# The 20th up tile of each FFN by seven block products

## The chip, the cores and the metric

The kernel runs on one core of a Trainium2 chip. Its metric is the device time of one execution in microseconds, from the launch to the end, as the median of several runs. The core has five engines that each work through their own list of instructions in order: TensorE (PE) for matmuls, VectorE (DVE) and ScalarE (ACT) for elementwise work, GpSimd (POOL), and SyncE (SP), which issues most of the loads. They wait for each other through semaphores. A matmul reads its operands from SBUF and adds into PSUM.

## The reference

A decoder of two layers over 512 tokens of width 1024, all in float32. Each layer has a mixer, a gated FFN with a causal convolution of width 3, and a gated embedding. The change lies in the FFN, which comes once in each layer:

```python
D_MODEL = 1024
SEQ = 512
D_FF = 2816
CONV_WIDTH = 3
...
def conv_ffn(xn, w_up, conv_w, conv_b, w_down):
    """Gated MLP with causal depthwise conv (width 3) between up-projection and activation."""
    S = xn.shape[1]
    h = xn @ w_up
    hp = jnp.pad(h, ((0, 0), (CONV_WIDTH - 1, 0), (0, 0)))
    c = conv_b + sum(hp[:, t:t + S] * conv_w[t] for t in range(CONV_WIDTH))
    g, u = jnp.split(c, 2, axis=-1)
    return (jax.nn.silu(g) * u) @ w_down
```

`w_up` is 1024 x 5632: 2816 columns for the gate `g` and 2816 for the line `u`. `w_down` is 2816 x 1024.

## The kernel before

**Tiles.** Activations lie with features on the 128 partitions and the 512 tokens along the free axis. The FFN's 2816 hidden features are 22 tiles of 128, numbered from 0, so that the 20th is tile 19. An up tile computes 128 gate rows and 128 line rows from the eight feature blocks of the input. Every float32 operand is split into a high and a low half (`wh` and `wl` for weights), and a product is three matmuls: high by high, high by low, low by high (`mm3`, L234).

**Two forms of an up tile.** The plain form (`up`) is 2 x 8 x 3 = 48 matmuls of 512 columns, into two PSUM tiles `up`. The form by seven block products (`woven_up`) treats gate and line rows, pairs of feature blocks, and the two halves of the tokens as a 2 x 2 by 2 x 2 block matrix product and forms it with seven products where eight are usual. Each product is 4 x 3 matmuls of 256 columns, so 84 in all. They go into PSUM tiles `ux` and `uy`, in the order 1, 2, 6, 5, 7, 3, 4. Between them ScalarE copies `ux` out into `gate` and `line` (L790, L794, L550) and half of `uy` into `side` (L796); a product that adds to a PSUM tile again waits for that copy. VectorE then finishes `line` (L803) and `gate` (L804). For its operands it needs sums of weight blocks, which VectorE forms in `weave` (L163, wide, then L164 and L165, half as wide), and sums of input blocks, made once for an FFN.

**Weights.** SP loads the weights of an up tile (128 x 2048, 1 MB) into one of three staging buffers, used in turn, by L173 (`wraw`). A tile by block products takes the next buffer as well, for its sums (`wsum`). A buffer is free for the next load or sum when the last split out of it is done. The weights are then split in units of at most 1024 columns: ScalarE casts the high half (`wh`, L203), VectorE subtracts for the low half (`wl`, L204). A plain tile has two units of 1024; a tile by block products has three of 1024 (blocks, sums, sums) and one of 512. There are four `wh` and four `wl` buffers, so that a unit can be split when TensorE is done with the unit four before it. TensorE takes the units in order.

**After an up tile**, `gated` runs the convolution: ScalarE scales by one tap (`c`, L753), VectorE adds two taps for gate and two for line (L755), ScalarE takes the silu (L761), VectorE multiplies (L762), and the product is split by ScalarE and VectorE into `act` high (L311) and low (L312).

**Parts.** The 22 tiles are handled in three parts, 0 to 7, 8 to 15 and 16 to 21. After each part come the down products of that part's hidden features. In the last part tile 16 is computed during the down products before it, then tiles 17 to 21 follow one another, then the down products in the plain form: four chunks of 36 matmuls each, whose weights are 128 x 1536 each (`d`, `wraw<-in_w_down`). The first chunk takes `act` 16 to 20 for both of its PSUM tiles and only then `act` 21. The scheduler sets the order of the instructions on each engine from the program's order and its own estimates; the order stays fixed at run time.

**The tables.** `UPS` (L23) names the tiles by block products. `ASIDE` (L24) names those among them whose `gate` and `line` lie in a free activation buffer, by its number, and not in the two common ones (`hs`). `turn` (L141) says which of the three staging buffers the first load takes.

The lines that the change and the steps of the prediction touch, cut short:

```python
    def staged(name):
        tags = state["tags"]
        r = wp.tile([P, 2 * UNIT], F32, tag=f"r{tags[state['turn'] % len(tags)]}", bufs=1, name=name)
        state["turn"] += 1
...
        def up(j, later=False):
            if j in UPS:
                return woven_up(j, later)
...
            head, tail = (ap.tile([P, S], F32, tag=f"a{y}{ASIDE[j]}", name=f"{x}{j}") if j in ASIDE else
                          tp.tile([P, S], F32, tag="hs", name=f"{x}{j}") for x, y in (("gate", "h"), ("line", "l")))
```

Of the kernel before, what the change touches and what calls it, by code (L numbers as in the profile page):

```python
# [19 lines left out]
NJ = FF // P  # L20
PARTS = [(0, 8), (8, 16), (16, 22)]
WOVEN = 2
UPS = (8, 9, 10, 12, 14, 16, 17, 18, 20, 21)  # L23
ASIDE = {9: 7, 17: 7, 20: 6}  # L24
PAIRS = 4
SLOTS = 9
N = S // 2
# [25 lines left out]
def tile_yoco(ctx: ExitStack, tc: tile.TileContext, t, out: bass.AP, out_b: bass.AP):  # L53
# [13 lines left out]
    def psum(name):  # L67
        return mmp.tile([P, S], F32, tag="mm", name=name)
# [35 lines left out]
    def plan_ups(l, j0, j1):  # L104
        for j in range(j0, j1):
            (plan_woven if j in UPS else plan_cols)(t["w_up"][l, j : j + 1], 1, *((0, KD) if j in UPS else (KD,)))

# [30 lines left out]

    units = [(i, q, lo, n) for i, p in enumerate(pieces) for q, (lo, n) in enumerate(p[2])]
    raws, ready, splits, sums = {}, {}, {}, {}  # L140
    state = {"raw": 0, "unit": 0, "next": 0, "tags": [0, 1, 2], "turn": 3, "pt": 0, "sent": {}}  # L141

    def behind(ins, front):

# [578 lines left out]
    def ffn(l, norm, nxt):  # L723
# [6 lines left out]
# [3 lines that stand above are left out]
            parts = chunk(256, KD)  # L733
            pss = [psum(f"up{j}_{s}") for s in range(2)]
            if j:
                for s in range(2):
                    mm3(pss[s], parts, xs, s * P)
            else:
                for k, ((wh, wl, off), (xh, xl)) in enumerate(zip(parts, xs)):
                    for x, both in ((xh, (wh, wl)), (xl, (wh,))):  # L740
                        for s, ps in enumerate(pss):
                            for w in both:
                                nc.tensor.matmul(ps, w[:, off + s * P : off + (s + 1) * P], x,  # L743
                                                 start=k == 0 and x is xh and w is wh, stop=k == KD - 1 and x is xl)
            return pss if later else gated(j, pss)
# [34 lines left out]
        def woven_up(j, later):  # L780

            product = products(ins)
            n = PAIRS * P
            chain, other = psum(f"ux{j}")[:, first], psum(f"uy{j}")
            head, tail = (ap.tile([P, S], F32, tag=f"a{y}{ASIDE[j]}", name=f"{x}{j}") if j in ASIDE else
                          tp.tile([P, S], F32, tag="hs", name=f"{x}{j}") for x, y in (("gate", "h"), ("line", "l")))
            side = tp.tile([P, N], F32, tag="sq", name=f"side{j}")
            w = unit()
            product(1, chain, w, 0)
            behind(box["silu"], nc.scalar.copy(head[:, first], chain))  # L790
            product(2, other[:, first], w, n)
            w = unit()
            product(6, chain, w, 0, first=False)
            nc.scalar.copy(head[:, second], chain)  # L794
            product(5, other[:, second], w, n)
            nc.scalar.copy(side, other[:, second])  # L796
            w = unit()
            product(7, chain, w, 0, first=False)
            minus(tail[:, second], chain)
            product(3, other[:, second], w, n, first=False)  # L800
            product(4, chain, unit(), 0, first=False)
            minus(tail[:, first], chain)
            nc.vector.tensor_sub(tail[:, second], tail[:, second], side)  # L803
            nc.vector.tensor_add(head, head, other)  # L804
            return (head, tail) if later else gated(j, (head, tail))
# [821 lines left out]
```

## Time and profile before

| | |
|---|---|
| median of 3 runs | 1101.53 us |
| lowest, highest | 1100.87, 1101.94 us |
| the profiled execution, its own time | 1102.24 us |
| its span, first to last instruction | 1100.5 us |
| tiles 17 to 21 in the first FFN | 415.63 to 467.12 us |
| tiles 17 to 21 in the second FFN | 963.76 to 1015.24 us |
| granted TensorE clock, mean | 0.998 |

The busy line of the page gives for each engine its busy time, the share of the span and the number of instructions. The chain that ended last is followed back from the last instruction: its shares say which engine set the time. A view of waits says who waited for whom: total, times, longest, in us. A row in order of time has the start, the length, the engine, the line and the operation with its output and inputs, and in brackets the idle time before it and what ended that. Neighbours on VectorE and ScalarE overlap a little at start and end, and a matmul's length is its time through the array, so the start-to-start time says what an instruction costs.

### The profile page before, as it was taken

The page shows a single profiled execution, that of the slowest core. Times are in us where ns is not written, and L with a number is a line of the kernel's source. Part 1 is how long each engine was busy: PE and PEld are TensorE (multiplying, and loading weights), DVE is VectorE, ACT ScalarE, POOL GpSimd, SP SyncE. Part 2 cuts the span into 40 slices and gives each one's busy share as a digit, 9 for nine tenths or more (in the row PEclk, how much of TensorE's full clock was granted, in tenths as well). Part 3 has the DMA queues.
Part 4 walks back from the last instruction along what each step waited for, and adds up shares of the span by engine and source line. Part 5 has one row for each costly group of instructions (what it writes and reads, how often), then busy time and mean ns, then how long its engine had stood idle before and what let it go on. Part 6 is the DMA issues. An engine that isn't in the chain of part 4 may idle for free.

```text
span 1100.5 us, 17400 instructions
## 1 busy us (share of the span) xinstructions
PE 1091.2 (99%) x6557; PEld 973.3 (88%) x6557; DVE 934.4 (85%) x1490; ACT 667.4 (61%) x1163; POOL 155.9 (14%) x228
## 2 busy tenths in 40 slices
PE   9999999999999999999999999999999999999997
PEld 7888988889998999988888887888899989999886
DVE  5598789888799978877988997798887999798796
ACT  5745665556676656655656775565566666566544
POOL 1100300002200030021114442000022000300200
PEclk9999999999999999999999999999999999999999
DMA  8621784126833388353234226441278333974634
GB/s 299 127 91 43 195 270 144 49 77 137 190 115 116 91 175 252 124 187 111 67 87 134 78 58 228 174 153 39 77 162 164 116 115 92 205 221 144 201 95 96
DMA packets 52692, 151.32 MB, mean 137 GB/s; under 512 B 13624, under 2 KB 21568, under 8 KB 42112
## 3 DMA queue, kind: packets, MB, share of 16 engines
q1 hardware_dynamic: 40560, 128.77, 36.5%
q0 software_dynamic: 10480, 16.78, 10.1%
q10 hardware_dynamic: 1568, 4.65, 1.1%
q8 instruction: 51, 0.84, 0.3%
q14 instruction: 33, 0.27, 0.1%
HBM read 116.89 MB, written 25.18 MB: 129 GB/s over the span
## 4 chain that ended last, share of the span: by engine, by line
PE 93%; DVE 2%; DMA 2%; issue 1%; ACT 1%; SPq 0%; POOLq 0%; POOL 0%; ACTq 0%; DVEq 0%
PE up L234 22%; PE ux L234 10%; PE dx L234 10%; PE uy L234 8%; PE dy L234 7%; PE q L234 4%; PE gate L234 4%; PE u L234 4%; PE o L234 4%; PE d L234 3%; PE up L743 2%; PE pv L1316 1%; PE v L244 1%; PE v L246 1%; PE v L245 1%
## 5 line engine op out<-in xcount | busy, mean ns | idle before, releaser
L204 DVE TENSOR_TENSOR wl<-wraw,wh 128x1024 fp32r<-128x1024 f32 (+2 forms) x198 | 219.1, 1110 | 49.8 <-ACT wh L203 47.4
L203 ACT CAST wh<-wraw 128x1024 fp32r<-128x1024 f32 (+2 forms) x197 | 183.6, 938 | 110.6 <-PE up L234 26.1
L204 DVE TENSOR_TENSOR wl<-wsum,wh 128x1024 fp32r<-128x1024 f32 x80 | 97.8, 1227 | 38.9 <-ACT wh L203 37.3
L203 ACT CAST wh<-wsum 128x1024 fp32r<-128x1024 f32 x80 | 84.1, 1051 | 38.0 <-PE uy L234 12.9
L755 DVE SCALAR_TENSOR_TENSOR c<-up,vec,c 128x511 f32<-128x511 f32 (+1 forms) x96 | 71.2, 746 | 2.5 <-ACT c L753 1.9
L594 POOL DMA_DIRECT2D saved<-side x16 | 13.9, 870 | 401.2 <-ACT side L550 401.2
L234 PE MATMUL up<-nf10h,wh 128*128 128x512 f32 x176 | 68.5, 389 | 0.0
L234 PE MATMUL up<-nf00h,wh 128*128 128x512 f32 x176 | 68.5, 389 | 0.0
L234 PE MATMUL up<-nf10l,wh 128*128 128x512 f32 x176 | 68.5, 389 | 0.0
L234 PE MATMUL up<-nf00l,wh 128*128 128x512 f32 x176 | 68.5, 389 | 0.0
L234 PE MATMUL up<-nf00h,wl 128*128 128x512 f32 x176 | 68.4, 389 | 0.0
L234 PE MATMUL up<-nf10h,wl 128*128 128x512 f32 x176 | 68.2, 389 | 0.0
L753 ACT ACTIVATE c<-up,vec 128x512 f32<-128x512 f32 x48 | 37.0, 775 | 34.2 <-PE up L234 29.0
L163 DVE TENSOR_TENSOR wsum<-wraw 128x1024 f32<-128x1024 f32 x40 | 48.9, 1223 | 0.8
L234 PE MATMUL ux<-t,wh 128*128 128x256 f32 x240 | 45.8, 283 | 0.0
L234 PEld LDWEIGHTS up<-nf00h,wl 128*128 128x128 f32 x176 | 33.0, 188 | 6.9
L234 PEld LDWEIGHTS up<-nf10h,wl 128*128 128x128 f32 x176 | 33.0, 188 | 6.8
L234 PEld LDWEIGHTS up<-nf10l,wh 128*128 128x128 f32 x176 | 33.1, 188 | 6.8
L234 PEld LDWEIGHTS up<-nf00l,wh 128*128 128x128 f32 x176 | 33.0, 188 | 6.8
L234 PEld LDWEIGHTS up<-nf10h,wh 128*128 128x128 f32 x176 | 33.1, 188 | 6.6
L234 PEld LDWEIGHTS up<-nf00h,wh 128*128 128x128 f32 x176 | 33.0, 188 | 6.6
L234 PEld LDWEIGHTS ux<-t,wh 128*128 128x128 f32 x240 | 37.4, 192 | 0.0
(738 smaller groups left out, 3693.0 us busy)
## 6 DMA issues: line engine op xcount, KB each, us to landing
wraw<-in_w_up SPq DMA_DIRECT2D x44, 1024.0 KB, 5.5
wraw<-in_w_down SPq DMA_DIRECT2D x16, 1024.0 KB, 4.9
wraw<-in_w_gate SPq DMA_DIRECT2D x8, 1024.0 KB, 5.7
wraw<-in_w_down SPq DMA_DIRECT2D x8, 768.0 KB, 4.4
wraw<-in_w_u SPq DMA_DIRECT2D x4, 1024.0 KB, 9.4
wraw<-in_w_out SPq DMA_DIRECT2D x4, 1024.0 KB, 5.0
saved<-head POOLq DMA_DIRECT2D x16, 256.0 KB, 4.9
saved<-rest POOLq DMA_DIRECT2D x16, 256.0 KB, 7.4
```

Of the source, the lines that this page charges most:

```text
L163: nc.vector.tensor_add(s[:, 0::3], g[:, 1:2].to_broadcast([P, 2, k, P]), g[:, 0::3])
L203: cast = nc.scalar.copy(hi, src)
L204: state["split"] = splits[u] = cast, nc.vector.tensor_sub(low, src, hi.bitcast(F32))
L234: return [nc.tensor.matmul(ps, w, x, start=first and j == 0, stop=last and j == len(todo) - 1, skip_group_check=onto) for j, (w, x) in enu ...
L244: nc.tensor.matmul(ps, xh[:, s], wh[:, a:b], start=st, stop=False)
L245: nc.tensor.matmul(ps, xl[:, s], wh[:, a:b], start=False, stop=False)
L246: nc.tensor.matmul(ps, xh[:, s], wl[:, a:b], start=False, stop=en)
L594: box["onto"] = nc.gpsimd.dma_start(x, y, accum_op=ALU.add)
L743: nc.tensor.matmul(ps, w[:, off + s * P : off + (s + 1) * P], x, start=k == 0 and x is xh and w is wh, stop=k == KD - 1 and x is xl)
L753: nc.scalar.activation(c, ps, AF.Identity, bias=v("conv_b", l * 2 * NJ + col), scale=cw[2])
L755: ins = nc.vector.scalar_tensor_tensor(c[:, tap:], ps[:, : S - tap], cw[2 - tap], c[:, tap:], op0=ALU.mult, op1=ALU.add)
L1316: nc.tensor.matmul(ps, lhs, rhs, start=j == 0, stop=j == len(todo) - 1)
```

## The change

Tile 19 joins the tiles by block products, in both FFNs. With it all five tiles from 17 to 21 have that form. Tile 19 takes the aside buffer 6, and tile 20 moves from 6 to 7. As tile 19 now takes two staging buffers, the first turn is set one lower, so that what follows the first FFN meets the same buffers as before.

```diff
--- before.py
+++ after.py
@@ -20,8 +20,8 @@
 NJ = FF // P
 PARTS = [(0, 8), (8, 16), (16, 22)]
 WOVEN = 2
-UPS = (8, 9, 10, 12, 14, 16, 17, 18, 20, 21)
-ASIDE = {9: 7, 17: 7, 20: 6}
+UPS = (8, 9, 10, 12, 14, 16, 17, 18, 19, 20, 21)
+ASIDE = {9: 7, 17: 7, 19: 6, 20: 7}
 PAIRS = 4
 SLOTS = 9
 N = S // 2
@@ -138,7 +138,7 @@
 
     units = [(i, q, lo, n) for i, p in enumerate(pieces) for q, (lo, n) in enumerate(p[2])]
     raws, ready, splits, sums = {}, {}, {}, {}
-    state = {"raw": 0, "unit": 0, "next": 0, "tags": [0, 1, 2], "turn": 3, "pt": 0, "sent": {}}
+    state = {"raw": 0, "unit": 0, "next": 0, "tags": [0, 1, 2], "turn": 2, "pt": 0, "sent": {}}
 
     def behind(ins, front):
```

The scheduler orders the stretch anew. Three places follow; the rows are in the engine's order, and the number behind a name says which tile (`gate18`, `c17_0`: tile 18, tile 17, gate) or which unit (`wl123`) or load (`wraw46`, tile 19's in both) it is.

VectorE, first FFN, while TensorE is in tile 18, before: tile 17's line taps and product, tile 19's two units, then the sums of tile 20.

```order
L755 SCALAR_TENSOR_TENSOR c17_1_4566<-line17_4447,vec_84,c17_1_4566 128x511
L755 SCALAR_TENSOR_TENSOR c17_1_4566<-line17_4447,vec_84,c17_1_4566 128x510
L762 TENSOR_TENSOR a17_4570<-a17_4570,c17_1_4566 128x512
L204 TENSOR_TENSOR wl123_4622<-wraw46_4619,wh123_4621 128x1024
L312 TENSOR_TENSOR act17l_4574<-a17_4570,act17h_4573 128x512
L204 TENSOR_TENSOR wl124_4652<-wraw46_4619,wh124_4651 128x1024
L163 TENSOR_TENSOR wsum47_4684<-wraw47_4680 128x2x512
L803 TENSOR_TENSOR line18_4588<-line18_4588,side18_4589 128x256
L164 TENSOR_TENSOR wsum47_4684<-wsum47_4684,wraw47_4680 128x512
L204 TENSOR_TENSOR wl125_4683<-wraw47_4680,wh125_4682 128x1024
L165 TENSOR_TENSOR wsum47_4684<-wsum47_4684,wraw47_4680 128x512
L804 TENSOR_TENSOR gate18_4587<-gate18_4587,uy18_4586 128x512
```

The same place with the change:

```order
L755 SCALAR_TENSOR_TENSOR c17_1_4566<-line17_4447,vec_84,c17_1_4566 128x511
L163 TENSOR_TENSOR wsum46_4623<-wraw46_4619 128x2x512
L755 SCALAR_TENSOR_TENSOR c17_1_4566<-line17_4447,vec_84,c17_1_4566 128x510
L164 TENSOR_TENSOR wsum46_4623<-wsum46_4623,wraw46_4619 128x512
L762 TENSOR_TENSOR a17_4570<-a17_4570,c17_1_4566 128x512
L165 TENSOR_TENSOR wsum46_4623<-wsum46_4623,wraw46_4619 128x512
L204 TENSOR_TENSOR wl123_4622<-wraw46_4619,wh123_4621 128x1024
L312 TENSOR_TENSOR act17l_4574<-a17_4570,act17h_4573 128x512
L204 TENSOR_TENSOR wl124_4656<-wsum46_4623,wh124_4655 128x1024
L803 TENSOR_TENSOR line18_4588<-line18_4588,side18_4589 128x256
L804 TENSOR_TENSOR gate18_4587<-gate18_4587,uy18_4586 128x512
L204 TENSOR_TENSOR wl125_4685<-wsum46_4623,wh125_4684 128x1024
```

The three sums of tile 19 now stand between tile 17's taps, its product and the first unit; after that unit 124 is a split of sums, and the sums of tile 20 come only after tile 18's taps.

ScalarE, in the same place, before: a copy of tile 18, tile 17's `act`, unit 124, the copy `side18`, and on.

```order
L794 COPY gate18_4587<-ux18_4585 128x256
L311 CAST act17h_4573<-a17_4570 128x512
L203 CAST wh124_4651<-wraw46_4619 128x1024
L796 COPY side18_4589<-uy18_4586 128x256
L550 ACTIVATE line18_4588<-ux18_4585 128x256
L203 CAST wh125_4682<-wraw47_4680 128x1024
```

And with the change:

```order
L794 COPY gate18_4587<-ux18_4585 128x256
L203 CAST wh124_4655<-wsum46_4623 128x1024
L311 CAST act17h_4573<-a17_4570 128x512
L796 COPY side18_4589<-uy18_4586 128x256
L550 ACTIVATE line18_4588<-ux18_4585 128x256
L203 CAST wh125_4684<-wsum46_4623 128x1024
```

The cast of unit 124 now reads the sums and stands ahead of tile 17's `act`; both stand ahead of the copy `side18`.

ScalarE at the end of the part, before: unit 134 is the second half of the first down chunk's weights, 135 and 136 those of the second (`wraw50`).

```order
L794 COPY gate21_4928<-ux21_4926 128x256
L311 CAST act20h_4922<-a20_4919 128x512
L796 COPY side21_4930<-uy21_4927 128x256
L203 CAST wh134_4992<-wraw49_4960 128x768
L550 ACTIVATE line21_4929<-ux21_4926 128x256
L203 CAST wh135_5023<-wraw50_5021 128x768
L753 ACTIVATE c21_0_5042<-gate21_4928,vec_84 128x512
L550 ACTIVATE line21_4929<-ux21_4926 128x256
L203 CAST wh136_5061<-wraw50_5021 128x768
L753 ACTIVATE c21_1_5046<-line21_4929,vec_84 128x512
L761 ACTIVATE a21_5050<-c21_0_5042 128x512
L311 CAST act21h_5053<-a21_5050 128x512
```

With the change the numbers of the units are two higher (137 and 138 are the second chunk's, 139 and 140 the third's):

```order
L203 CAST wh137_5081<-wraw50_5079 128x768
L311 CAST act20h_4980<-a20_4977 128x512
L550 ACTIVATE line21_4987<-ux21_4984 128x256
L753 ACTIVATE c21_0_5100<-gate21_4986,vec_84 128x512
L753 ACTIVATE c21_1_5104<-line21_4987,vec_84 128x512
L203 CAST wh138_5119<-wraw50_5079 128x768
L761 ACTIVATE a21_5108<-c21_0_5100 128x512
L203 CAST wh139_5179<-wraw51_5177 128x768
L311 CAST act21h_5111<-a21_5108 128x512
L203 CAST wh140_5183<-wraw51_5177 128x768
```

The cast of the second chunk's first unit has moved ahead of `act20h`, of the last copy for `line21` and of both `c21`, and one unit of the third chunk stands ahead of `act21h`. On VectorE the order there is the same: the split of unit 137, `act20` low, the four taps of tile 21, unit 138, the product, unit 139, `act21` low; before, `act20` low and both units of the first chunk were done ahead of the second chunk's first unit, and the third chunk's first unit came after `act21` low. SP issues the third chunk's load (`wraw51`) ahead of the second's (`wraw50`) in both: the third goes into the buffer of tile 21's sums, the second into that of tile 21's weights, and the next tile's weights or sums always wait for the split before them in that buffer.

## The prediction

> **What bounds the kernel now.** I read the busy line first, then the chain that ended last and TensorE's waits, then the four stretches of the part in which the changed tile lies, and last that part's instructions one by one.
>
> ```profile
> PE 1091.2 (99%) x6557; PEld 973.3 (88%) x6557; DVE 934.4 (85%) x1490; ACT 667.4 (61%) x1163; POOL 155.9 (14%) x228
> PE 93%; DVE 2%; DMA 2%; issue 1%; ACT 1%; SPq 0%; POOLq 0%; POOL 0%; ACTq 0%; DVEq 0%
> ```
> ```profile
> PE idle L283 <- DVE minus_half L286: 1.1, 1, 1.1
> PE gt L246 <- DVE wl L204: 0.2, 1, 0.2
> PE sc L1248 <- PE sc L1249: 0.2, 1, 0.2
> ```
>
> TensorE is on 93% of the chain, and all its waits in 1100.5 us are these three, none of them in an FFN's last part. So time can come only from fewer or shorter matmuls, and every wait that the change makes for TensorE is paid in full, since no later idle time can take it up. VectorE is the one to watch. Stretches by rows (start:end, length, then busy time of PE, PEld, DVE, ACT, POOL): tiles 17 and 18, tile 19, tiles 20 and 21, the down products; tile 19 and tiles 20 and 21 again in the second FFN.
>
> ```profile
> 415.63:436.00 20.37, 20.37 (x171) 20.21 (x170) 18.95 (x25) 14.64 (x25) 1.75 (x2) 1.00 0.78 229
> 436.00:446.91 10.91, 10.91 (x50) 9.01 (x49) 10.17 (x14) 5.87 (x9) 0.00 (x0) 1.00 0.36 148
> 446.91:467.12 20.21, 20.21 (x169) 20.15 (x168) 17.81 (x25) 14.14 (x25) 0.41 (x2) 1.00 0.46 157
> 467.12:499.80 32.68, 32.68 (x147) 27.04 (x145) 23.94 (x30) 18.09 (x28) 6.71 (x5) 1.00 0.55 193
> 984.13:995.04 10.91, 10.91 (x51) 9.00 (x50) 10.16 (x14) 5.87 (x9) 0.00 (x0) 1.00 0.35 147
> 995.04:1015.24 20.20, 20.20 (x169) 20.14 (x168) 18.10 (x25) 14.36 (x25) 0.53 (x1) 1.00 0.46 154
> ```
>
> VectorE is busy 10.17 us of the plain tile's 10.91: it pays there what tiles 17 and 18 left over. The plain tile 19 is VectorE's rest, and the change takes it away.
>
> **TensorE's gain.** The plain tile is 48 matmuls of 512 columns, the block form 7 x 12 of 256. From the chain, in order of time (start, length):
>
> ```profile
> 436.16 10.91 PE up L234 x48
> 422.98 1.59 PE uy L234 x12
> 424.57 2.87 PE ux L234 x24
> ```
>
> Twelve of 256 take 1.44 us (2.87 for 24), so a block tile takes 7 x 1.44 = 10.05; where a product first waits for the copy of `side` it is 0.15 more (1.59). Tiles 20 and 21 together took 20.21. So the gain is 10.91 - 10.05 = 0.86 us at best, some 0.75 with that small wait, for each FFN: 1.5 to 1.7 us in all. [...]
>
> **VectorE's added work.** Start-to-start times are what counts, since neighbours overlap by some 0.09 us:
>
> ```profile
> 427.41 0.69 DVE L204 TENSOR_TENSOR wl<-wraw,wh 128x512 fp32r<-128x512 f32 x1
> 428.01 0.75 DVE L755 SCALAR_TENSOR_TENSOR c<-gate,vec,c 128x510 f32<-128x510 f32 x1
> 428.67 1.53 DVE L755 SCALAR_TENSOR_TENSOR c<-line,vec,c 128x511 f32<-128x511 f32 x2
> 430.31 0.69 DVE L762 TENSOR_TENSOR a<-a,c 128x512 f32<-128x512 f32 x1
> 430.92 1.22 DVE L204 TENSOR_TENSOR wl<-wraw,wh 128x1024 fp32r<-128x1024 f32 x1
> 433.89 1.22 DVE L163 TENSOR_TENSOR wsum<-wraw 128x1024 f32<-128x1024 f32 x1
> 435.02 0.42 DVE L803 TENSOR_TENSOR line<-line,side 128x256 f32<-128x256 f32 x1
> 435.36 0.68 DVE L164 TENSOR_TENSOR wsum<-wsum,wraw 128x512 f32<-128x512 f32 x1
> 435.96 1.22 DVE L204 TENSOR_TENSOR wl<-wraw,wh 128x1024 fp32r<-128x1024 f32 x1
> 437.10 0.68 DVE L165 TENSOR_TENSOR wsum<-wsum,wraw 128x512 f32<-128x512 f32 x1
> 437.70 0.68 DVE L804 TENSOR_TENSOR gate<-gate,uy 128x512 f32<-128x512 f32 x1
> 438.37 0.75 DVE L755 SCALAR_TENSOR_TENSOR c<-line,vec,c 128x511 f32<-128x511 f32 x1
> ```
>
> So a wide sum (L163) takes 1.13, a 1024 split 1.14, a 512 sum, split or product 0.60, a tap (L755) 0.66, L803 0.34, L804 0.67. Tile 19 gains one L163, an L164 and L165 (2.33 together), one and a half more splits (1.74) and L803 and L804 (1.01): 5.1 us. Its taps cost the same from either source. ScalarE gains 1.5 casts and five short copies, and has the idle time for them (5.87 busy of 10.91).
>
> Is VectorE late by that? From tile 17's line tap (428.67 in both orders) to the last split of tile 21's weights the new order has 10 taps (6.60), 3 L163 (3.39), 6 sums (3.60), 9 splits of 1024 (10.26) and 3 of 512 (1.80), 3 products and 3 `act` splits (3.60), 3 L803 (1.02) and 3 L804 (2.01): 32.28. Without one wait it ends at 428.67 + 32.28 + 0.09 = 461.04. Before:
>
> ```profile
> 458.64 0.69 DVE L204 TENSOR_TENSOR wl<-wraw,wh 128x512 fp32r<-128x512 f32 x1
> 459.36 0.33 SPq L173 DMA_DIRECT2D wraw<-in_w_down  x1
> 461.42 0.96 DVE L204 TENSOR_TENSOR wl<-wraw,wh 128x768 fp32r<-128x768 f32 x1
> 462.30 0.68 DVE L762 TENSOR_TENSOR a<-a,c 128x512 f32<-128x512 f32 x1
> 466.07 0.83 ACT L203 CAST wh<-wraw 128x768 fp32r<-128x768 f32 x1 [1.14 <-DMA wraw<-in_w_down]
> 473.14 0.69 DVE L312 TENSOR_TENSOR act21l<-a,act21h 128x512 fp32r<-128x512 f32 x1 [0.69 <-ACT act21h L311]
> 474.18 0.39 PE L234 MATMUL d<-act21l,wh 128*128 128x512 f32 x1
> 475.32 0.39 PE L234 MATMUL d<-act16h,wh 128*128 128x512 f32 x1
> ```
>
> There (rows of four engines in order of time) it ended at 459.33, with some waits in it. VectorE's waits from 426.75 to 473.9 before, apart from two for the last `act`:
>
> ```profile
> DVE wl L204 <- ACT wh L203: 2.4, 6, 0.8
> DVE c L755 <- ACT c L753: 0.2, 1, 0.2
> ```
>
> Bounds: no wait, 1.7 us late; all these 2.6 us again, 4.3 late. I take 0.3 us, 461.3, since an engine that runs behind seldom finds its input missing: 2.0 us late. The weights of tiles 20 and 21 still come in time: by the same count tile 21's first split ends at 455.3, and TensorE, which starts tile 20 at 446.91 - 0.86 and needs 10.15 for it, wants that split two matmuls later, at 456.4.
>
> **What is late next.** The second down product's weights load into the buffer that this split frees; SP issued them 0.03 us after it (459.36) and ScalarE waited for them until 466.07, 6.71 us. Now issue is at 461.3 and landing at 468.0. In the new order the cast of these weights stands on ScalarE ahead of act20h, of line21's second copy and of both c21; behind it on VectorE come its split, act20l, four taps, a split, the product, a split and act21l. From landing: cast 0.83, splits 3 x 0.88 (461.42 to 462.30), act20l and product 1.20, taps 2.64, act21l 0.69, in all 8.0 (before: 473.83 - 466.07 = 7.8). So act21l ends at 476.0. TensorE meets act21l's first matmul at 474.18 now, 0.35 after act21l was ready, and after the change would be there at 473.4 or so: the slack is gone and the wait decides. The next chunk starts 475.32 - 474.18 = 1.14 after that matmul, at 477.2 in place of 475.32: **1.9 us later**. The two early waits (side of tile 18, behind act17h on ScalarE, at most 0.6; act20l, some 0.7) lie ahead of this one and are swallowed by it.
>
> In the second FFN the cast was held by TensorE and not by the load, issued at 1007.49:
>
> ```profile
> 1007.49 0.33 SPq L173 DMA_DIRECT2D wraw<-in_w_down  x1
> 1013.89 0.83 ACT L203 CAST wh<-wraw 128x768 fp32r<-128x768 f32 x1 [0.84 <-PE uy L234]
> ```
>
> So that load took 6.4 us at most, and its FFN loses 0.3 less, 1.6. Bounds of the load: the same load's median over all is 4.4 us (the row below); at that it lands at 465.7, act21l is there at 473.7 and each FFN gains some 0.5. I stay near 6.7, since the third chunk's load is still issued just ahead of it and shares the engines.
>
> ```profile
> wraw<-in_w_down SPq DMA_DIRECT2D x8, 768.0 KB, 4.4
> ```
>
> **Sum.** 1.9 + 1.6 = 3.5 us over the profiled execution's 1102.24 (span 1100.5): 1105.7. That execution is 0.71 over the median of 1101.53, so the predicted median is **1105.0**. Without any VectorE wait it is 0.6 less; with all 2.6 in each FFN 4.6 more, 1109.6. What comes after the part follows TensorE and moves with it. The other number in the table only turns the names of the three staging buffers; it costs nothing, as the rotation is as long as before.
>
> **Rivals.** *VectorE keeps up*: the load comes in 4.4 to 5 us, or VectorE's starts move closer together, act21l is ready before 473.4, and the full 1.5 to 1.7 is gained: 1099.9. For it: VectorE is busy only 46.9 us (18.95 + 10.17 + 17.81) of the 51.5 of the five tiles, and 5.1 more, less the overlaps, would fit. Against: laid end to end, overlaps taken off, its rows already end 1.7 late, for they also carry tile 17's rest. 13%. [...] *Half and half*: the load is quick, but ScalarE, with the side copy of tile 18 queued behind act17h, holds TensorE 0.6 us, and act20l a little; the gain is eaten and nothing more, 1101 to 1103. 16%. *VectorE falls behind inside the tiles*: its old waits recur on top (4.3 us late), tile 21's splits come after 456.4 and TensorE waits for them already there, from the point at which VectorE has waited over 1.1 us by 455; 3 to 4 us an FFN, 1108 to 1110. 8%.
>
> **How the numbers follow.** The forecast has 60%, its own range 1103.5 to 1107.5. The range for 8 in 10 takes in the half-way case and part of the gain: 1100.0 to 1108.2. About 0.2%, 2.2 us, is what a measurement of this kernel can tell from no change. Slower by more than that (over 1103.7): nearly all of the forecast and the last rival, 0.65. Within it: the first and third rivals and a bit of the forecast, 0.31. Faster: 0.04.
>
> **What would show it.** In the profile after: tile 19 as 84 matmuls in 10.05 to 10.2 us; VectorE's last split for tile 21 some 2 us later than 459.3; a cast of `wraw<-in_w_down` held by its load until about 468; and, new in TensorE's waits, `d` held by act20l and act21l, some 2.5 us in each FFN. The forecast is wrong if act21l is ready before TensorE gets there, if TensorE waits for `wl` inside tiles 19 to 21, or if time is lost outside the two parts.

## The result and the profile after

| | before | after |
|---|---|---|
| median of 8 runs each, same chip | 1101.57 us | 1104.26 us |
| lowest, highest | 1100.87, 1102.37 | 1103.26, 1107.18 |
| the profiled execution, its own time | 1102.24 | 1107.18 |
| its span | 1100.5 | 1105.5 |

The ratio is 1.0029, with a 95% interval of 1.002 to 1.0039: slower by 2.7 us. Five of the eight runs after lie at 1103.3 to 1104.3 and three at 1106.4 to 1107.2; the profiled one is the slowest of them.

First the stretches of the profile after that answer to those of before: tiles 17 to 21, the down products to the next matrix, both again in the second FFN, and gt's first two token blocks up to the matmul np1ms. A row has start:end, length, busy time of PE, PEld, DVE, ACT, POOL (with counts), the granted clock, DMA share and GB/s.

```profile
415.46:466.48 51.02, 50.87 (x423) 50.40 (x421) 49.57 (x67) 35.20 (x62) 4.76 (x4) 1.00 0.55 170
466.48:500.48 34.00, 33.31 (x146) 26.88 (x145) 24.76 (x32) 19.63 (x30) 6.86 (x6) 1.00 0.58 202
964.47:1015.50 51.03, 50.88 (x422) 50.41 (x421) 49.56 (x67) 35.19 (x62) 2.08 (x3) 1.00 0.54 168
1015.50:1049.70 34.20, 33.31 (x146) 26.89 (x145) 26.16 (x37) 19.88 (x32) 7.27 (x6) 1.00 0.62 203
1049.70:1061.65 11.95, 10.36 (x38) 7.75 (x37) 11.50 (x18) 8.25 (x12) 0.00 (x0) 0.86 0.30 97
```

The last three of these before the change:

```profile
963.76:1015.24 51.48, 51.48 (x386) 49.36 (x385) 47.21 (x62) 34.62 (x58) 2.28 (x3) 1.00 0.55 176
1015.24:1047.92 32.68, 32.68 (x147) 27.04 (x145) 26.88 (x37) 18.09 (x30) 6.93 (x5) 1.00 0.61 199
1047.92:1056.64 8.72, 8.48 (x38) 6.52 (x36) 8.27 (x14) 8.16 (x12) 0.00 (x0) 1.00 0.30 108
```

The five tiles are shorter, by 0.47 us in the first FFN (51.49 before) and 0.45 in the second. The down products are longer, by 1.32 and 1.52. So a last part costs 0.85 and 1.07 us net. And gt, behind the second FFN, takes 11.95 us where it took 8.72: 3.2 us more, in a place that the prediction did not look at. What lies between and around these stretches is equal within 0.2 us.

TensorE's waits after (total, times, longest, in us). The two of `idle` (1.1) and `sc` (0.2), which are there before too, are left out; the third of before was `gt` for `wl`, 0.2:

```profile
PE d L234 <- ACT act21h L311: 1.4, 2, 0.7
PE gt L244 <- ACT wh L203: 1.1, 1, 1.1
PE gt L246 <- DVE wl L204: 0.5, 1, 0.5
PE d L234 <- DVE act20l L312: 0.2, 1, 0.2
PE uy L234 <- ACT side L796: 0.2, 1, 0.2
```

Two new places: `d` waits for the two last activations, and `uy` of tile 18, shortly, for the copy `side`. And gt waits longer for its own weights.

**At the end of a last part** (loss A below). Rows in order of time, of VectorE, SP, ScalarE and TensorE:

```profile
460.34 0.68 DVE L204 TENSOR_TENSOR wl<-wraw,wh 128x512 fp32r<-128x512 f32 x1
461.06 0.33 SPq L173 DMA_DIRECT2D wraw<-in_w_down  x1
467.14 0.84 ACT L203 CAST wh<-wraw 128x768 fp32r<-128x768 f32 x1 [2.43 <-DMA wraw<-in_w_down]
467.88 0.62 ACT L311 CAST act20h<-a 128x512 fp32r<-128x512 f32 x1
473.80 0.62 ACT L311 CAST act21h<-a 128x512 fp32r<-128x512 f32 x1 [0.71 <-DVE a L762]
474.47 0.74 PE L234 MATMUL d<-act21h,wh 128*128 128x512 f32 x2 [0.69 <-ACT act21h L311]
474.55 0.68 DVE L312 TENSOR_TENSOR act21l<-a,act21h 128x512 fp32r<-128x512 f32 x1
475.05 0.40 PE L234 MATMUL d<-act16h,wh 128*128 128x512 f32 x1
475.75 0.39 PE L234 MATMUL d<-act21l,wh 128*128 128x512 f32 x1
```

The last split of tile 21's weights ends at 461.02, where it ended at 459.33. SP issues the second down chunk's load 0.04 us after it, ScalarE stands 2.43 us before that load's cast, act20h and all that leads to act21h stand behind the cast, and TensorE is at act21h's matmul first. TensorE's own order has changed here too: behind act21h's two matmuls stand three of the next chunk (475.05 to 475.75) and only then act21l's, so that act21l, ready at 475.23, is not waited for, and the units are not taken quite in order here. Before, act21l's first matmul came straight behind act21h's first (474.18 and 473.96).

**At the end of the second FFN** (loss B). The same engines there:

```profile
1021.42 0.95 DVE L204 TENSOR_TENSOR wl<-wraw,wh 128x768 fp32r<-128x768 f32 x1
1022.40 0.38 SPq L173 DMA_DIRECT2D wraw<-in_w_gate  x1
1022.85 1.35 SPq L1408 DMA_DIRECT2D row_m<-lines  x2
1032.42 0.41 ACT L1419 CAST rows<-row_m 128x256 fp32r<-128x256 f32 x1 [3.44 <-DMA row_m<-lines]
1053.65 0.50 PE L244 MATMUL gt<-wh,np10h 128*128 128x512 f32 x1 [1.07 <-ACT wh L203]
1054.91 0.50 PE L246 MATMUL gt<-wl,np10h 128*128 128x512 f32 x1 [0.52 <-DVE wl L204]
```

Before the change, the gate load, the first cast of the bias rows, and gt's only wait:

```profile
1018.12 0.38 SPq L173 DMA_DIRECT2D wraw<-in_w_gate  x1
1028.08 0.41 ACT L1419 CAST rows<-row_m 128x256 fp32r<-128x256 f32 x1 [1.54 <-DMA row_m<-lines]
1051.49 0.50 PE L246 MATMUL gt<-wl,np10h 128*128 128x512 f32 x1 [0.24 <-DVE wl L204]
```

The first gate load waits in SP's queue for a buffer that a split of the second chunk frees at 1022.37; before, it went out at 1018.12. The two loads of the bias rows stand behind it. ScalarE, in order, waits for them 3.44 us (1.54 before), with gt's casts behind, and TensorE waits 1.07 and 0.52 us in the middle of gt (before, once 0.24). Then this, in stretches of 2 us: of the rows, the second number is PE's busy time, and after the five engines stands the granted clock.

```profile
1053.00:1055.00 2.00, 0.83 (x3) 0.39 (x3) 1.90 (x3) 2.00 (x3) 0.00 (x0) 1.00 0.52 207
1055.00:1057.00 2.00, 2.00 (x7) 1.58 (x8) 2.00 (x3) 1.91 (x5) 0.00 (x0) 0.70 0.00 0
1057.00:1059.00 2.00, 2.00 (x6) 1.57 (x5) 2.00 (x5) 1.98 (x4) 0.00 (x0) 0.50 0.00 0
1059.00:1061.00 2.00, 2.00 (x10) 1.61 (x9) 2.00 (x4) 0.77 (x1) 0.00 (x0) 0.95 0.06 13
```

Behind the waits the clock falls to one half, and a matmul of 512 columns takes 0.43 us from start to start in place of 0.23 (seven and six in 2 us, then ten).

### The profile page after: what moved, and what is told of

It reads as the page before. It is cut to its first block, busy times and chain, and to the rows that moved or that the text cites. A ratio compares the mean times of both kernels' runs of the same rounds, so it can differ in the third digit from the quotient of the medians.

```text
span 1105.5 us, 17582 instructions
## 1 busy us (share of the span) xinstructions
PE 1092.8 (99%) x6629; PEld 975.1 (88%) x6629; DVE 941.2 (85%) x1504; ACT 672.4 (61%) x1177; POOL 159.2 (14%) x228
## 4 chain that ended last, share of the span: by engine, by line
PE 88%; DVE 4%; DMA 3%; ACT 2%; issue 2%; SPq 0%; POOLq 0%; POOL 0%; ACTq 0%; DVEq 0%
PE up L234 20%; PE dx L234 10%; PE ux L234 9%; PE uy L234 8%; PE dy L234 7%; PE q L234 4%; PE gate L234 4%; PE u L234 4%; PE o L234 4%; PE d L234 3%; PE up L743 2%; PE pv L1316 1%; ACT wh L203 1%; DVE wl L204 1%; DMA wraw<-in_w_v 1%
## 5 line engine op out<-in xcount | busy, mean ns | idle before, releaser
L204 DVE TENSOR_TENSOR wl<-wsum,wh 128x1024 fp32r<-128x1024 f32 x84 | 102.6, 1226 | 37.8 <-ACT wh L203 36.2
L755 DVE SCALAR_TENSOR_TENSOR c<-up,vec,c 128x511 f32<-128x511 f32 (+1 forms) x88 | 65.1, 745 | 2.0 <-ACT c L753 1.5
L234 PE MATMUL up<-nf10l,wh 128*128 128x512 f32 x160 | 62.3, 389 | 0.0
L234 PE MATMUL up<-nf10h,wh 128*128 128x512 f32 x160 | 62.3, 389 | 0.0
L234 PE MATMUL up<-nf00h,wh 128*128 128x512 f32 x160 | 62.3, 389 | 0.0
L234 PE MATMUL up<-nf00l,wh 128*128 128x512 f32 x160 | 62.3, 389 | 0.0
L234 PE MATMUL up<-nf00h,wl 128*128 128x512 f32 x160 | 62.1, 389 | 0.0
L234 PE MATMUL up<-nf10h,wl 128*128 128x512 f32 x160 | 62.0, 389 | 0.0
L234 PE MATMUL ux<-t,wh 128*128 128x256 f32 x264 | 50.6, 284 | 0.0
L234 PE MATMUL ux<-t,wl 128*128 128x256 f32 x132 | 37.3, 283 | 0.0
```

The source lines that it names most:

```text
L204: state["split"] = splits[u] = cast, nc.vector.tensor_sub(low, src, hi.bitcast(F32))
L234: return [nc.tensor.matmul(ps, w, x, start=first and j == 0, stop=last and j == len(todo) - 1, skip_group_check=onto) for j, (w, x) in enu ...
L755: ins = nc.vector.scalar_tensor_tensor(c[:, tap:], ps[:, : S - tap], cw[2 - tap], c[:, tap:], op0=ALU.mult, op1=ALU.add)
```

## The experiments

The theory: loss A (the second chunk's late load and its place on ScalarE) and loss B (SP's queue, the bias rows, gt's casts), each by order, not by the amount of work. Rival 1: VectorE has some 5 us more to do in each FFN, and that must come out whatever the order. Rival 2: the clock falls anywhere in some runs, and the rest is noise. All stage lengths come from the starts of TensorE's rows in each kernel's profiled execution:

| kernel | median (its before), us | 1st FFN, tile 17 to the next matrix | 2nd FFN, the same | gt to np1ms |
|---|---|---|---|---|
| before | 1101.57 | 84.17 | 84.16 | 8.72 |
| after | 1104.26 (1101.57) | 85.02 | 85.23 | 11.95 |
| e1 first FFN only | 1103.58 (1101.76) | 85.21 | 84.25 | 8.59 |
| e2 second FFN only | 1104.04 (1101.76) | 84.16 | 85.82 | 9.40 |
| e3 tile 20 plain | 1103.41 (1101.76) | 84.66 | 84.69 | 8.41 |
| e4 act21 first | 1101.86 (1101.76) | 83.89 | 83.95 | 9.39 |
| e5 rows by POOL | 1103.75 (1101.97) | 85.69 | 85.25 | 8.16 |
| e6 before, act21 first | 1101.85 (1101.97) | 84.17 | 84.18 | 8.81 |
| e7 e4 and side18 first | 1102.17 (1101.97) | 83.86 | 83.84 | 9.52 |
| e8 after, one run more | 1105.37 (1101.97) | 85.05 | 85.11 | 9.77 |
| e9 split first | 1102.96 (1101.59) | 83.95 | 83.95 | 12.05 |
| e10 e9 with e5 and e7 | 1102.00 (1101.59) | 83.91 | 85.41 | 8.16 |
| e11 before, late cast | 1103.58 (1101.59) | 84.16 | 84.16 | 10.60 |
| e12 e10, rows' casts put back | 1100.53 (1102.05) | 83.92 | 83.90 | 8.16 |

**e1 and e2: one FFN at a time.** The tables are made for each layer:

```diff
-UPS = (8, 9, 10, 12, 14, 16, 17, 18, 19, 20, 21)
-ASIDE = {9: 7, 17: 7, 19: 6, 20: 7}
+UPS = ((8, 9, 10, 12, 14, 16, 17, 18, 19, 20, 21),
+       (8, 9, 10, 12, 14, 16, 17, 18, 20, 21))
+ASIDE = ({9: 7, 17: 7, 19: 6, 20: 7}, {9: 7, 17: 7, 20: 6})
```

This is e1; e2 has the two entries of each in the other order, and the first turn at 3.

> Tile 19 is woven in the first FFN only; the second FFN is as before the change. Theory (two losses: A, at the end of each last part, the late load and cast of the second down chunk stand ahead of act20 and act21; B, at the end of the second FFN, the late split holds SP's queue, the bias rows land late, ScalarE is held and gt's casts are late): only A of the first FFN, +0.85 us, so 1102.0 to 1102.8 against 1101.6; no wait of gt for a cast over 0.5 us and a granted clock of 1.00 after gt's start. Rival 1 (each FFN simply pays for 5.1 us more work of VectorE, half of the whole loss each): about 1103. Rival 2 (the extra over +1 is TensorE's clock falling at any place in some runs): runs up to 1107 here too.

> Tile 19 is woven in the second FFN only. Theory: A of the second FFN, +1.1 us, and all of B, +0.9 to +3.2 us more, so 1103 to 1106, with a wait of gt for its unit's cast of about 1 us at the end of the second FFN, and single runs in two groups. Rival 1: about 1103, as the first FFN alone. Rival 2: as the first FFN alone.

e1: 1103.58 us, ratio 1.0017 (1.0008 to 1.0027), ten runs from 1102.7 to 1104.4. e2: 1104.04, ratio 1.0021 (1.0012 to 1.003), 1102.1 to 1106.0. The places are as the theory has them: in e1 the first FFN has the 1.0 us and the second and gt are as before; in e2 the second FFN has 1.7 us, gt 0.7. The size of e1 is a miss: its median is 1.8 us over before, its stages add up to 1.0. The interval (0.9 to 3.0 us) holds both, so the medians of these two alone don't tell the theory from rival 1; the stages do. No run of e1 reached 1105, so the runs over 1106 need the second FFN, which speaks against rival 2. (That the clock falls in each of them is not shown: see e8.)

**e3: as many block tiles as before, the plain one at 20.**

```diff
-UPS = (8, 9, 10, 12, 14, 16, 17, 18, 19, 20, 21)
-ASIDE = {9: 7, 17: 7, 19: 6, 20: 7}
+UPS = (8, 9, 10, 12, 14, 16, 17, 18, 19, 21)
+ASIDE = {9: 7, 17: 7, 19: 6}
```

The first turn is at 3, as in before.

> As many woven tiles as before the change: 19 is woven and 20 is plain. Theory: VectorE catches up in the plain tile 20, the second chunk's split comes about as early as before, so within 0.6 us of before, 1101.0 to 1102.2, with no wait of the second FFN's gt for a cast over 0.5 us. Rival 1: as before too (the same count of work). A rival of place (weaving tile 19 itself costs something): +1 us or more.

1103.41 us, ratio 1.0014 (1.0005 to 1.0023): a miss, the rival of place holds. Tiles 17 to 21, then the down products, in the first FFN:

```profile
415.47:467.45 51.98, 51.83 (x386) 49.41 (x385) 46.88 (x62) 34.67 (x58) 2.52 (x4) 1.00 0.58 183
467.45:500.13 32.68, 32.68 (x146) 27.04 (x145) 23.69 (x30) 17.89 (x28) 6.73 (x5) 1.00 0.53 191
```

The down products are back at 32.68 and gt at 8.41: with a plain tile late in the part, A and B are gone, as expected. But the same tiles take 0.5 us more than before in each FFN (51.98 against 51.49). Of this, 0.31 is a gap ahead of the matmul at 433.65, at the start of product 3 of tile 18 (the sixth in the order of the seven), which adds to the half of `uy` that the copy `side` reads. It stands in every FFN up to here in which tile 19 is a block tile, and in none of before. Call it loss C; in after it cuts the tiles' gain from 0.78 to 0.47. It costs after nothing in the end, since `d` then stands before act21h, whose time the load sets (e5); it counts where A is gone. Where the other 0.2 and the rest of e3's median come from stays open.

**e4: the second chunk's first cast and split behind act21's.** In the down products' loop:

```diff
+            if c == 0:
+                halves = box["halves"]
...
+                for ins, front in zip(splits[state["next"]], halves):
+                    behind(ins, front)
```

`halves` are act21's cast and split. With it SP issues the bias rows' loads ahead of the first gate load, and TensorE does all of act21's matmuls ahead of the second chunk's.

> After the change, with the second down chunk's first unit cast and split behind act21's halves (SP's bias-row loads then go out ahead of the first gate load). Theory: A and B both gone, each FFN keeps the 0.5 us that TensorE's shorter tiles brought: 1100.3 to 1101.2, no wait of d for act21h over 0.3 us, no wait of gt for a cast over 0.5 us. Rival 1 (VectorE's additional work must come out whatever the order): as after, 1103.3 to 1104.5. A new wait: the chunk's second unit of d comes at its own cast, which is now late; where that is late, a wait of d for wh of the second chunk at its start shows it, and the time lies between.

1101.86 us against 1101.76, ratio 1.0 (0.9992 to 1.0009), which is over the 1101.2 hoped for but no longer slower than before, and this with VectorE busy as long as after (943.0 us against 941.2): rival 1 falls. Its stretches, as above, and what is left of the waits of `d` and gt:

```profile
415.31:466.32 51.01, 50.86 (x422) 50.39 (x421) 49.65 (x67) 35.85 (x63) 4.75 (x4) 1.00 0.55 172
466.32:499.20 32.88, 32.88 (x146) 26.97 (x145) 24.73 (x32) 19.45 (x30) 7.82 (x7) 1.00 0.60 209
1047.16:1056.55 9.39, 8.79 (x38) 6.47 (x36) 8.94 (x15) 8.16 (x12) 0.00 (x0) 1.00 0.33 109
```
```profile
PE gt L246 <- DVE wl L204: 0.5, 1, 0.5
```

No wait of `d` is left and each FFN is 0.2 to 0.3 us shorter than before. But TensorE comes to gt 0.8 us earlier (1047.16 against 1047.92) and gt's casts don't: the gate loads go out at 1023.24 here. What the FFNs gain, gt gives back (9.39 against 8.72).

**e5: the bias rows' loads by POOL**, nothing else in the code of after changed (the scheduler then puts their small casts on ScalarE a little earlier):

```diff
-        nc.sync.dma_start(x.rearrange("p (m q) -> p m q", m=KD), lines[:, i, :].partition_broadcast(P))
+        nc.gpsimd.dma_start(x.rearrange("p (m q) -> p m q", m=KD), lines[:, i, :].partition_broadcast(P))
```

> After the change, with the loads of the bias rows (row_m from lines) issued by POOL instead of SP, so that they don't stand behind the first gate load. Theory: loss A stays (d to the next chunk 34.0 and 34.2 us), loss B goes: ScalarE waits under 1.6 us for row_m, gt's first wait for wh (1.1 us) is gone, gt to np1ms 8.7 to 9.5 us as in the other kernels and not 11.95; 1102.8 to 1103.6, no run over 1104.6, no granted clock under 1.00 after gt's start. Rival (the bias rows are innocent, gt's casts are late because d ended late): gt to np1ms stays over 10.5 us and runs over 1106 stay.

1103.75 us, ratio 1.0016 (1.0007 to 1.0025), a little over the 1103.6 expected at most. B is gone: gt takes 8.16 us, 0.56 less than before, at a clock of 1.00, TensorE never waits there, and the eleven runs lie between 1103.1 and 1104.5, none in the group over 1106. So the bias rows in SP's queue were the cause of B. That their casts moved as well is no rival: in e12 they stand where after had them, and gt takes the same 8.16 us. A is larger here than in after, 1.5 us in the first FFN:

```profile
461.23 0.33 SPq L173 DMA_DIRECT2D wraw<-in_w_down  x1
468.00 0.83 ACT L203 CAST wh<-wraw 128x768 fp32r<-128x768 f32 x1 [3.10 <-DMA wraw<-in_w_down]
```

The same load, issued 0.17 us later than in after, lands 0.86 later: 6.77 us against 6.08. A follows it, and d waits 0.58 us for act20l too. The record has eight FFNs with this order at the end of the part. With the load taken from its issue to the cast that waits for it, and each FFN against 84.17 or 84.16 before:

| kernel, FFN | after, 1st | e8, 1st | e8, 2nd | e1, 1st | after, 2nd | e5, 2nd | e5, 1st | e2, 2nd |
|---|---|---|---|---|---|---|---|---|
| the load, us | 6.08 | 6.15 | 6.19 | 6.26 | 6.28 | 6.32 | 6.77 | 6.94 |
| the FFN is longer by, us | 0.85 | 0.88 | 0.95 | 1.04 | 1.07 | 1.09 | 1.52 | 1.66 |

Each time the loss is the load's length less 5.21 to 5.28 us. In this order, then, that one load sets the size of A.

**e6: e4's edit on before**, as a control.

> Before the change, with the same edit as e4 (the second down chunk's first cast and split behind act21's halves). Theory: there was no wait to take away there, so as before or a little slower, 1101.3 to 1102.3; then e4 owes its time to the taking away of the change's waits. Rival: the edit is a gain by itself (the bias rows' loads earlier on SP): 1100.5 or less.

1101.85 us against 1101.97, ratio 0.9995 (0.9986 to 1.0005), with every stage within 0.1 us of before. The edit is no gain by itself; what it gave to after came from the change's own waits.

**e7: e4, and side18's copy ahead of act17h.**

```diff
-            nc.scalar.copy(side, other[:, second])
+            copied = nc.scalar.copy(side, other[:, second])
+            if j == 18:
+                behind(box["halves"][0], copied)
```

> e4, and also ScalarE's copy side18 ahead of its cast act17h. Theory (a third loss, C: a woven tile 19 brings a gap of 0.31 us at tile 18's seventh product, which waits for side18): tile 17 to d 50.7 us instead of 51.0 in each FFN; of the 0.3 us in the second FFN gt's last casts, which come with the gate load and the last sums, may take it back; 1101.2 to 1101.7. Rival: act17h comes later, and act17l with it, and something behind them waits: 51.0 or more.

1102.17 us, ratio 0.9999 (0.999 to 1.0007): no gain, and tiles 17 to 21 take 50.96 and 50.95 us, 0.05 less where 0.3 was expected. ScalarE and TensorE there:

```profile
430.85 1.05 ACT L203 CAST wh<-wsum 128x1024 fp32r<-128x1024 f32 x1 [1.20 <-DVE wsum L164]
431.81 0.36 ACT L800 COPY side<-uy 128x256 f32<-128x256 f32 x1
432.22 0.39 PE L234 MATMUL uy<-nf00h,wh 128*128 128x256 f32 x1
```

The copy is still queued behind the cast of tile 19's sums, which waits for VectorE. It does start 0.52 us earlier, counted from the start of product 7 (1.29 us behind it; in e4 1.81). But TensorE's order has changed with it: in e4 four matmuls of tile 19 stand ahead of the product that waits for the copy (432.69 to 433.17), and here none do, so TensorE comes to the copy some 0.48 us earlier too, and a gap of 0.26 is left of 0.31. So act17h was not the whole cause of C; moving the copy ahead of the cast of the sums wasn't tried.

**e8: after once more**, unchanged.

> After the change once more, for a second profile. Theory: the waits of d (0.69 us for act21h in each FFN, 0.2 for act20l) and of gt for its casts (1 to 2 us) are there in every execution; only the fall of the granted clock behind gt's wait tells 1103.3 to 1104.4 from 1106.4 to 1107.2. Should this run be near 1104, its clock after gt's start is 1.00 and gt to np1ms is 9.5 to 10.5 us instead of 11.95. Rival: runs near 1104 have no wait of gt at all.

One run, 1105.37 us, between the two groups of after's first eight runs. The same waits of d, and gt waits here too, 0.49 and 0.52 us; but the clock holds:

```profile
PE gt L246 <- DVE wl L204: 0.5, 1, 0.5
PE gt L244 <- ACT wh L203: 0.5, 1, 0.5
```
```profile
1053.00:1055.00 2.00, 1.11 (x4) 0.63 (x5) 1.90 (x3) 2.00 (x4) 0.00 (x0) 1.00 0.38 152
1055.00:1057.00 2.00, 2.00 (x10) 1.65 (x9) 2.00 (x4) 2.00 (x5) 0.00 (x0) 1.00 0.00 0
```

gt takes 9.77 us, 2.2 less than in the first profile: 0.6 of that is wait, 1.6 is the clock. So A and B with a full clock cost 0.88 + 0.95 + 1.05 = 2.9 us here, near the 2.7 of the medians, and the fall of the clock, where it comes, adds 1.6. What parts the two groups of runs is not settled by this: they lie some 3 us apart, and only one run of the upper group has a trace. The mean granted clock on record is 0.996 for that run, 0.998 and 0.997 for the other two of the upper group, and 0.998 or 0.999 for the five lower ones; e2's one run over 1106 has 0.999. A fall like the one seen takes 0.0015 off the mean (3.4 us at one half, of 1105), so some runs of the upper group may have none.

**e9: the load 1.0 us earlier.** Tile 20's two closing sums on VectorE go behind the last split of tile 21:

```diff
-            nc.vector.tensor_sub(tail[:, second], tail[:, second], side)
-            nc.vector.tensor_add(head, head, other)
+            closed = nc.vector.tensor_sub(tail[:, second], tail[:, second], side)
+            if j == 21:
+                for x in box["closed"]:
+                    behind(x, splits[state["next"] - 1][1])
+            box["closed"] = closed, nc.vector.tensor_add(head, head, other)
```

ScalarE's order stays; on TensorE one matmul of d slips in among tile 21's, so that the two stretches are taken together.

> After the change, with tile 20's two closing sums on VectorE (line20 and gate20, 0.4 and 0.6 us) behind the last split of tile 21, so that this split and with it the second down chunk's load start 1.0 us earlier; ScalarE's order stays. Theory (A is only how late that load starts): its cast starts about 466.2 instead of 467.14, the waits for act20l and act21h go, d to the next chunk 32.7 to 33.0 us in both FFNs instead of 34.0 and 34.2; the gate load behind it on SP goes out 1 us earlier too, and gt to np1ms falls from 9.8 or 11.95 to 9 to 10: 1101.3 to 1102.4, no run over 1104. Rival (VectorE's additional 5 us, not the load, hold act21): act21h is as late as before, d to the next chunk stays 33.8 or more, 1103.3 or more.

1102.96 us, ratio 1.0015 (1.0006 to 1.0024), runs from 1101.1 to 1106.9. A is gone: the load is issued at 459.86, 1.2 us earlier than in after, the cast is at 465.33 and waits for no load (0.57 us in the second FFN), no wait of d is left, and each FFN takes 83.95 us, 0.2 less than before. VectorE has the same work as in after: the order alone did it. B stayed, against what was expected, and the clock fell again:

```profile
415.20:499.15 83.95, 83.80 (x567) 77.34 (x565) 74.20 (x98) 55.35 (x92) 10.79 (x9) 1.00 0.56 187
1046.80:1058.85 12.05, 10.38 (x38) 7.73 (x36) 11.60 (x18) 8.24 (x12) 0.00 (x0) 0.86 0.31 96
```
```profile
PE gt L244 <- ACT wh L203: 1.1, 1, 1.1
PE gt L246 <- DVE wl L204: 0.5, 1, 0.5
```

The gate load goes out at 1019.35, 3 us earlier than in after and still 1.2 later than before, and ScalarE still waits 3.61 us for the bias rows behind it. e5 takes B away and leaves A, e9 takes A away and leaves B: they are two losses, with two ways to TensorE.

**e10: e9 with the edits of e5 and e7.**

> e9 with the edits of e5 (bias rows' loads by POOL) and of e7 (copy side18 ahead of act17h). Theory: 50.95 us from tile 17 to d, 32.7 to 33.0 from d to the next chunk, 8.2 to 9.0 from gt to np1ms: 0.5 us gained in each FFN, 1100.3 to 1101.2, faster than both kernels. Rival: with TensorE that much earlier the gate weights, which come at their own time, set gt's start: gt to np1ms 9.5 and 1101.5 to 1102.

1102.00 us, ratio 1.0002 (0.9993 to 1.001), not the 1100.3 to 1101.2 hoped for. The first FFN and gt are as hoped, 83.91 and 8.16, but the second FFN takes 85.41: d waits 1.41 us for act21h. The edit of e5 had let the scheduler put two casts of the bias rows ahead of tile 21's silu on ScalarE, and here their load was not there:

```profile
1019.62 0.82 ACT L1429 CAST rows<-row_m 1x256 fp32r<-1x256 f32 x2 [2.36 <-DMA row_m<-lines]
1021.85 0.62 ACT L311 CAST act21h<-a 128x512 fp32r<-128x512 f32 x1
```

**e11: a late cast in before.** The cast of gt's last unit goes behind the last np1sq, to make TensorE wait there:

```diff
     parts = chunk(S, KD)
+    behind(splits[state["next"] - 1][0], box["squared", KD - 1])
```

> Before the change, with the cast of gt's last unit on ScalarE behind the last np1sq, so that TensorE waits 2 to 3 us in the middle of gt, as it waited 1.07 and 0.52 in the profile of after, and for nothing else. If TensorE's waits of over a us there bring its clock down: a granted clock of about 0.5 to 0.7 for some 4 us behind the wait, matmuls of 512 columns at 0.43 instead of 0.23 us, and 3.5 to 5 us lost, 1105 to 1107, in all or many runs. If the fall in after's profile had nothing to do with the wait: clock 1.00, 2 to 3 us lost, 1103.5 to 1104.7.

1103.58 us, ratio 1.0019 (1.001 to 1.0028). The scheduler moved the wait: TensorE waits for np1quarter instead, behind gt's first blocks.

```profile
PE np1ms L388 <- DVE np1quarter L379: 1.8, 1, 1.8
```

In the profiled run the clock stays at 1.00 and 1.9 us are lost. But the ten runs lie in two groups, six up to 1103.6 and four at 1104.9 to 1105.2. The mean granted clock of the four is 0.997 each, that of the six 0.997 to 0.999, as is that of the runs of before beside them. That fits a clock that falls after such a wait in some executions; no run of the upper group has a trace, so it is argued and not shown.

**e12: e10 with the bias rows' casts where after had them**, behind the second np1sq:

```diff
-            nc.scalar.copy(whole[:, cols], a)
+            whole_cast = nc.scalar.copy(whole[:, cols], a)
+            if lows == 32:
+                behind(whole_cast, box["squared", 1])
...
-                    nc.scalar.copy(rows[q : q + 1, cols], a[q : q + 1])
+                    row_cast = nc.scalar.copy(rows[q : q + 1, cols], a[q : q + 1])
+                    if lows == 32:
+                        behind(row_cast, box["squared", 1])
```

> e10 with the four small instructions on the bias rows (three casts on ScalarE, one difference on VectorE) behind the second np1sq, as they stood in after; in e10 the scheduler had put two of them ahead of tile 21's silu in the second FFN, where d then waited 1.41 us for act21h. Theory: that wait goes, 83.9 us from tile 17 to gt in the second FFN as in the first instead of 85.4; gt comes 1.5 us earlier, and the gate weights' casts then set part of its start: gt to np1ms 8.2 if they keep up, 9.5 if they don't. Against before's 1101.6: 1100.3 if they keep up, 1101.6 if they don't. Rival (the wait for act21h had another cause): 85 us or more again, 1101.8 to 1102.3.

1100.53 us against 1102.05, ratio 0.9988 (0.9979 to 0.9997), eleven runs within 1100.0 to 1101.0: faster than both kernels, by little. Each FFN and gt:

```profile
415.16:499.08 83.92, 83.81 (x567) 77.34 (x565) 74.17 (x98) 55.40 (x92) 10.77 (x9) 1.00 0.57 186
962.75:1046.65 83.90, 83.79 (x566) 77.34 (x565) 78.52 (x107) 56.23 (x96) 11.63 (x10) 1.00 0.58 190
1046.65:1054.81 8.16, 8.16 (x37) 6.76 (x36) 8.05 (x12) 7.42 (x11) 0.00 (x0) 1.00 0.22 81
```

VectorE is busy 941.3 us as in after, and no wait of `d` or gt is left; of C a gap of 0.27 us is. The stages add up to 1.1 us of the 1.5 between the medians: 0.25 in each FFN is what is left of the block tile's gain, 0.56 is gt's, which the edits to the bias rows bring. Whether before would have that part without the change wasn't tried.

## Why the prediction was right, and where not

The sign and the size came out: 1105.0 was predicted, 1104.26 measured, inside the range and the forecast's own. That the size is so near is luck in part. The sum's only loss, A, was put at 3.5 us and cost 1.9 in the profile of after (0.85 + 1.07); the rest of the loss is B, which the sum didn't have.

- TensorE's gain: 0.75 to 0.86 us an FFN was predicted, 0.47 and 0.45 measured. The difference is C, the gap of 0.31 us at tile 18; the prediction named that wait, at most 0.6, and held that the later one swallows it. In after it does, as the load alone sets how late the FFN ends (e5). So the sentence that every wait of TensorE is paid in full doesn't hold for this one.
- VectorE's queue: the last split was to end at 461.04 without waits, 461.3 with. It ended at 461.02. From after's own first tap, at 428.51, the same count gives 460.88, and VectorE waited 0.16 us on the way. The count of instructions by their start-to-start times holds.
- The load: issue 0.04 us after the split, as said. Its 6.71 us were 6.08 in the first FFN, and the cast came at 467.14 and not at 468.0; in the second it took 6.28, where 6.4 at most was said. That is 0.6 and 0.1 of the sum's 1.9 and 1.6.
- What stands behind the cast: 8.0 us were counted from landing to the end of act21l, and it took 8.1 (467.14 to 475.23). In e5 the load landed at 468.00, as predicted, and act21l ended at 476.08 where 476.0 was said. Yet that FFN lost 1.52 us and not 1.9.
- The first step that failed is the one after it: "the slack is gone and the wait decides", the wait being act21l's. It took TensorE's order for unchanged. In the new order three matmuls of the next chunk, 0.70 us, stand between act21h's and act21l's. `d` waited 0.7 us for act21h in each FFN and 0.2 once for act20l, never for act21l, where some 2.5 us for act20l and act21l was said. By e5's table a load of 6.71 us costs 1.46 in this order, 0.4 less than the sum has.
- The second: "What comes after the part follows TensorE and moves with it." It does not at the end of the second FFN. The same late splits on VectorE hold a buffer, SP's queue stands at the gate load, the bias rows behind it land late, and ScalarE stops with gt's casts behind it. That costs 1.05 us (e8) and, where the clock falls after it, 3.2 (the first profile). "If time is lost outside the two parts" was given as what would make the forecast wrong, and by the mechanism it did.
- Of the rivals, "VectorE keeps up" is what e9 and e12 make of the kernel by hand, short of the full gain. "Half and half", which the chances count as the third rival, had the side copy, at twice its size (0.6 for 0.31), and act17h is one of two things that hold it (e7). TensorE never waited for weights inside tiles 19 to 21.

## What to carry to other kernels

When an edit makes an engine later, follow every buffer that it frees, through the load that waits for it, past the loads queued behind that load, to the next in-order engine that meets one of them; here the second loss lay 30 us behind the first. Read the new order of the engine that sets the time as well, and not only that of the others: here it filled part of the wait. VectorE, busy 85% of the time before, could take more work once what it frees came early in its order: e9 moved two sums, 1.0 us together, behind one split, and a loss of about a microsecond in each FFN was gone. After an edit that takes away one dependence, look again at what the scheduler moved ahead (e10 against e12).

## What the hardware did that was not expected

The granted clock of TensorE fell to one half after short waits. In after it followed gaps of 1.23 and 0.69 us within 2.5 us, 1.9 together, in e9 of 1.30 and 0.69, 2.0 together; with 0.66 and 0.69 (e8), or with 1.95 at once (e11's profile), it stayed at 1.00. By the granted clock of the 2 us stretches shown above (0.70, 0.50 and 0.95) it stood at one half for 3.4 us in after, which costs 1.6; in e9 the three stretches from 1052 to 1058 have 0.78, 0.50 and 0.87, again 3.4 us.

What sets the fall off, and what ends it, these runs don't show. The longest gap alone does not tell the profiles apart: 1.23 and 1.30 us with the fall, 1.95 without. And of the two executions of the same kernel that have a trace, one has it (after) and one not (e8).

The load of the second down chunk's weights, 768 KB, took 6.08 to 6.94 us in the eight FFNs of e5's table, 6.08 and 6.15 in the first FFN of two executions of the same kernel (after and e8), and TensorE paid for the difference.
